# The first feature block's conditioning sums as matmuls with the conditioning column

## The chip, the cores and the metric

One NeuronCore of a Trainium2 chip runs the whole program in one launch. The metric is device time in microseconds of one execution; a number for a kernel is the median of several executions. The profile is one further execution, recorded with its own time.

## The reference

Two layers of an encoder trunk over a sequence of 1024 rows of 1024 features. What matters here is the start of the first layer: the input rows are normalized, scaled and shifted by vectors that depend on a conditioning vector `c`, and multiplied with `w_in`.

```python
def rmsnorm(x, g):
    xf = x.astype(jnp.float32)
    y = xf * lax.rsqrt(jnp.mean(xf * xf, axis=-1, keepdims=True) + NORM_EPS)
    return (y * g.astype(jnp.float32)).astype(x.dtype)

def modulate(h, shift, scale):
    return h * (1 + scale[:, None, :]) + shift[:, None, :]

c_act = jax.nn.silu(c)                         # 1024 numbers
...
    mod = c_act @ ada_w[l] + ada_b[l]          # 1024 x 6144
    sh_m, sc_m, g_m, sh_f, sc_f, g_f = jnp.split(mod, 6, axis=-1)
    h = modulate(rmsnorm(x, norm_g[l, 0]), sh_m, sc_m)
    if l < N_A:
        y = short_conv_mixer(h, conv_in_w[l], conv_w[l], conv_b[l], conv_out_w[l])
...
def short_conv_mixer(h, w_in, w_conv, b_conv, w_out):
    bcx = h @ w_in                             # 1024 x 1024 times 1024 x 3072
    b_gate, c_gate, xh = jnp.split(bcx, 3, axis=-1)
...
```

## The kernel before

Features are cut into eight blocks `k` of 128 (`KD = 8`), rows into eight tiles of 128, and the sequence into two halves of 512. `conv_phase` opens the program. Its first half loops over the eight feature blocks; for each block it needs three things on TensorE:

- The normalized rows of the block, turned to features by rows: `turn(k, half)` does four transposes of 128 x 128 into one PSUM tile `tp`. The rows come from `norm_x(0)`: for each of the four row tiles ACT squares and sums (`junk`, L364) and takes a root (L366), VectorE takes the reciprocal (L371) and scales the rows in place (`y`, L1175).
- The block's scale and shift, `sh[k]`, two columns of 128 numbers. They are sums over all 1024 conditioning numbers: `ada_cols` loads the block's columns of `ada_w` (tile `aw`, four DMAs of half the rows of either scale or shift), `ada_sum` multiplies and adds its eight row blocks with `csil`, the silu of `c`, in eight VectorE operations (L1083, then seven of L1085) into the tile `av`; `ada_end` sums `av` over its 128 partitions by a matmul with a column of `ones` (L1092, one for the scale and one for the shift), and two VectorE operations make `sh` of it (L1093, L1095). Blocks 0 and 1 have sums of their own, 256 wide; from block 2 on, two blocks share eight operations, 512 wide.
- The block's weights, `weights(k)`: 128 rows of `w_in` with 768 columns (tile `w`), split into a high and a low part by `split_w` (ACT L240, VectorE L241).

`scaled` then makes the block's operand: ACT writes it twice from `tp` (L1106), rounded into `slot` (hi) and in full into `q`; VectorE subtracts (L1107), which leaves the low part, lo. `products` multiplies weights and operand: three groups `g` for each of two output blocks `m`, each group three matmuls of 512 columns (low x high, high x low, high x high, through `mm`, L237). Between the two `m` of a block `k` stands `scales(k + 1)`, with its `ada_end` ahead of everything else in it.

The order on TensorE and on the SP queue is that of the code (`pinned`); on ACT it is that of the code in `norm_x(0)`. On VectorE the order is that of the code inside `beside`, and a scheduler's elsewhere. Each engine runs its instructions strictly in that order. SP issues the loads: `c`, four row tiles of `x`, then for blocks 0 and 1 `aw` and `w`, then two blocks at a time; `aw` has three buffers.

`c` is read as a column tile, element by element, into `craw` by the first DMA; ACT takes its exponential at once (L201) and VectorE makes `csil` of it. After Exp, ACT takes a first root (L228), so that its table for roots is there before `norm_x(0)`. Gains and biases come as rows (`vrows`, `brows`) and are turned by TensorE in `feature_rows` (L1059).

Of the kernel before, what the change touches and what calls it, by code (L numbers as in the profile page):

```python
# [8 lines left out]
F32 = mybir.dt.float32  # L9
# [3 lines left out]
ALU = mybir.AluOpType  # L13
# [4 lines left out]
P = 128  # L18
# [90 lines left out]
def trunk_kernel(ctx: ExitStack, tc: tile.TileContext, x, c, ada_w, ada_b, norm_g, conv_in_w, conv_w,  # L109
# [5 lines left out]
    def nm(s):  # L115
        uid[0] += 1
        return f"{s}_{uid[0]}"
# [73 lines left out]
    def ld(out_, in_):  # L191
        nc.sync.dma_start(out_, in_)
# [4 lines left out]

    csil = cp.tile([P, KD], F32, name="csil")
    craw = cp.tile([P, KD], F32, name="craw")
    ld(craw, c.rearrange("o (k p) -> p (o k)", p=P))  # L200
    nc.scalar.activation(csil, craw, AF.Exp, scale=-1.0)  # L201
    nc.scalar.dma_start(cs, consts[:, :C_T])

    rows_ = raw_tile()
    vrows, brows, mrows = (rows_[:, i * P:(i + 1) * P] for i in range(3))
    nc.scalar.dma_start(vrows[0:64, :], norm_g.rearrange("l v (k p) -> (l v k) p", p=P))
    nc.scalar.dma_start(brows[0:96, :], ada_b.rearrange("l (k p) -> (l k) p", p=P))

# [14 lines left out]
    nc.vector.memset(eps_d, D * EPS)  # L223
    eps_1 = cp.tile([P, 1], F32, name="eps_1")
    nc.vector.memset(eps_1, EPS)
    vecs = cp.tile([P, VEC_ROWS], F32, name="vecs")
    bias = cp.tile([P, BIAS_ROWS], F32, name="bias")
    nc.scalar.activation(bias[:, 0:1], csil[:, 0:1], AF.Sqrt)  # L228

    def gain(l, v):  # L230
        return vecs[:, (l * 4 + v) * 8:(l * 4 + v) * 8 + 8]

# [2 lines left out]
    def mm(out_, lhs, rhs, first, last, more=False):  # L235
        for i, (a, b) in enumerate(((1, 0), (0, 1), (0, 0))):
            nc.tensor.matmul(out_, lhs[a], rhs[b], start=first and i == 0, stop=last and i == 2, skip_group_check=more)  # L237
# [2 lines left out]
        nc.scalar.activation(hi, src, AF.Copy)  # L240
        nc.vector.tensor_tensor(lo, src, hi.bitcast(F32), op=ALU.subtract)  # L241


    nc.vector.tensor_scalar(csil, csil, 1.0, None, op0=ALU.add)
    nc.vector.reciprocal(csil, csil)
    nc.vector.tensor_tensor(csil, csil, craw, op=ALU.mult)

    def ada_room(accp):
        return accp.tile([P, D], F32, tag="acc", name=nm("acc"), bufs=1)
# [782 lines left out]
    def conv_phase():  # L1032
# [20 lines left out]
            for t in range(4 * half, 4 * half + 4):  # L1053
                ld(xt[t], x0[t * P:(t + 1) * P, :])

        def feature_rows(src, *dst):
            p_ = tp_ps()
            n = src.shape[0]
            nc.tensor.transpose(p_[:, :n], src, ident[:n, :n])  # L1059
            o = 0  # L1060
            for d in dst:
                nc.vector.tensor_copy(d, p_[:, o:o + d.shape[-1]])
                o += d.shape[-1]
# [5 lines left out]
        def ada_cols(ks):  # L1069

            n = len(ks)
            raw = [st.tile([P, KD * 2 * P], F32, tag="aw", name=nm("aw"), bufs=3).rearrange(
                "p (i j m) -> p i j m", i=KD // n, j=2) for _ in range(n)]
            q = KD // 2
            for i in (0, q):
                for j, col in enumerate((D, 0)):
                    ld(raw[i * (n - 1) // q][:, i % (KD // n):i % (KD // n) + q, j, :],
                       w0[i * P:(i + q) * P, col + ks[0] * P:col + (ks[-1] + 1) * P].rearrange("(k p) m -> p k m", p=P))
            return [raw[i * n // KD][:, i % (KD // n)] for i in range(KD)]

        def ada_sum(ks, raw):
            acc = st.tile([P, 4 * P], F32, tag="av", name=nm("av"), bufs=2)[:, :len(ks) * 2 * P].rearrange("p (j m) -> p j m", j=2)
            nc.vector.tensor_scalar(acc, raw[0], csil[:, 0:1], None, op0=ALU.mult)  # L1083
            for i in range(1, KD):
                nc.vector.scalar_tensor_tensor(acc, raw[i], csil[:, i:i + 1], acc, op0=ALU.mult, op1=ALU.add)  # L1085
            for n, k in enumerate(ks):
                sums_[k] = acc[:, :, n * P:(n + 1) * P]

        def ada_end(k):
            p_ = tp_ps()  # L1090
            for j in range(2):
                nc.tensor.matmul(p_[:, j:j + 1], sums_[k][:, j, :], ones[:, 0:1], start=True, stop=True)  # L1092
            nc.vector.scalar_tensor_tensor(sh[k][:, 0:1], p_[:, 0:1], g1[:, k:k + 1], b1[:, k:k + 1], op0=ALU.mult,  # L1093
                                           op1=ALU.add)
            nc.vector.tensor_tensor(sh[k][:, 1:2], p_[:, 1:2], bias[:, k:k + 1], op=ALU.add)  # L1095
# [25 lines left out]
        def weights_split(raw):  # L1121
            room = len(ws) in order[:FIRST_KEPT]
            w = [wr[room].tile([P, 6 * P], F32R, tag="w" + part_, name=nm("w"), bufs=FIRST_KEPT if room else KD - FIRST_KEPT)
                 for part_ in "hl"]
            split_w(w[0], w[1], raw)
            return w

        late = []

        def products(w, k, half, m, acc, first, last):  # L1130
            for g in (1, 0, 2):
                mm(acc[m, g], [q[:, (2 * g + m) * P:(2 * g + m + 1) * P] for q in w], ops[("1", "2")[k // 4] + ("1", "2")[half]][k % 4],
                   first, last)

        kept_rows = [None, None]

# [36 lines left out]
        def norm_x(half):  # L1173
            for t in range(4 * half, 4 * half + 4):
                nc.vector.tensor_scalar(xt[t], xt[t], rroot(squares(nx, xt[t])), None, op0=ALU.mult)  # L1175
# [6 lines left out]
        with pinned([mybir.EngineType.PE, mybir.EngineType.SP]):  # L1182
            load_x(0)
            wraws, sums_, ws, turned = [], {}, [], {}

            def fetch(*ks):
                raw = ada_cols(ks)
                wraws.extend(weights(k) for k in ks)
                return ks, raw

            aws = [fetch(0), fetch(1)]
            feature_rows(vrows[:64, :], vecs[:, :64])
            feature_rows(brows[:96, :], bias[:, :96])
            nc.vector.tensor_scalar(g1, gain(0, 0), RMS, None, op0=ALU.mult)
            nc.vector.scalar_tensor_tensor(b1, bias[:, 8:16], 1.0, g1, op0=ALU.add, op1=ALU.mult)
            with pinned([mybir.EngineType.Activation]):
                norm_x(0)

            def scales(k, beside=None):
                ada_end(k)  # L1200
                if beside:
                    with pinned([mybir.EngineType.DVE]):
                        beside()
                scaled(k, turned.pop(k), old(k), ("11", "21")[k // 4])
                ws.append(weights_split(wraws[k]))

            ada_sum(*aws[0])
            turned[0] = turn(0, 0)
            scales(0, lambda: ada_sum(*aws[1]))
            turned[1] = turn(1, 0)  # L1210
            acc = banks6()
            for k in range(KD):
                if k % 2 == 0 and k + 2 < KD:
                    ada_sum(*fetch(k + 2, k + 3))
                elif k + 2 == KD:
                    load_x(1)
                    later_rows()
                products(ws[k], k, 0, 0, acc, k == 0, k == KD - 1)
                if k + 1 < KD:
                    scales(k + 1)  # L1220
                else:
                    evict(0, 0, acc)
                    norm_x(1)
                products(ws[k], k, 0, 1, acc, k == 0, k == KD - 1)
                if k + 2 < KD:
                    turned[k + 2] = turn(k + 2, 0)
            evict(1, 0, acc)
            st.release()
            cB = pool("cB", "right")
            for n, t_ in zip(("t1", "t2"), slots_of(cB, 2)):  # L1230
                ops[n] = as_quarter(t_)
            ops["t3"], ops["t4"] = [], {}
            ready = []

            def next_half():
                k = order[len(ready)]
                second_half(k, turn(k, 1))
                ready.append(k)

            next_half()  # L1240
            next_half()
            acc = banks6()
            summed = 0
            for n, k in enumerate(order):
                products(ws[k], k, 1, 0, acc, n == 0, n == KD - 1)
                if len(ready) < KD:
                    next_half()
                elif n == KD - 2:
                    feature_rows(mrows[:VEC_ROWS - 64 + 16, :], vecs[:, 64:VEC_ROWS], bias[:, 96:BIAS_ROWS])
                products(ws[k], k, 1, 1, acc, n == 0, n == KD - 1)  # L1250
                if summed < 4 and summed in order[:n + 1] and summed + 4 in ready:
                    sums(summed)
                    summed += 1
                if n == FIRST_KEPT - 1:
                    wr.pop().release()
                    up = pool("up", "right")
                    begun = load_pair(conv_in_w[0], 4 + 1)
                    begun += (up_split(up, begun[0]),)
            for m in range(2):
                evict(m, 1, acc)  # L1260
# [746 lines left out]
```

## Time and profile before

| | us |
|---|---|
| median of 3 executions | 2083.88 (2081.64 to 2084.84) |
| the profiled execution | 2082.84 |
| its span in the trace | 2081.1 |
| first product (`one<-slot,w`, L237) starts | 20.61 |
| first half's last products of `mm<-slot,w` start | 65.71 |

The span is the time from the first to the last recorded instruction; 1.7 us of the execution lie around it. Granted clock over the span is 0.998. A row of the timeline has start, length, engine, line, operation, tiles (out<-in), shape and count, and in brackets how long the engine sat idle before it and what ended that. Rows that follow each other are merged, their length then reaching from the first one's start to the last one's end. One f32 matmul of 128 x 128 with one column leaves two records, so the two matmuls of an `ada_end` stand as `x4`. In rows of stages the numbers behind the length are busy time and count for each engine.

### The profile page before, as it was taken

To read this page: it belongs to the slowest core of one execution; us is meant where nothing else is said; L and a number is where in the kernel's file an instruction comes from. 1 tells how busy PE (TensorE), PEld (TensorE's weight loads), DVE (VectorE), ACT (ScalarE), POOL (GpSimd) and SP (SyncE) were. 2 spreads that over 40 slices of the span, in tenths; PEclk is the share of its full clock that TensorE was granted. 3 is DMA by queue.
4 is the path that set the end of the run, shared out by engine and by line. 5 is a ranking of instruction groups with operands and counts; after the bars stand their busy time and mean duration, and the time that the engine had idled before them with its cause. 6 is when DMAs were issued, how large, how long until landed. Compare 5 with 4: busy or idle time off the path is not lost.

```text
span 2081.1 us, 25026 instructions
## 1 busy us (share of the span) xinstructions
PE 2036.0 (98%) x9447; PEld 1683.6 (81%) x9447; DVE 1554.1 (75%) x2070; ACT 1083.9 (52%) x1547; POOL 5.3 (0%) x13
## 2 busy tenths in 40 slices
PE   6999999999999999999999999999999999999998
PEld 4788878878878788888878888888788888888886
DVE  7687877885776569978788978878976764567477
ACT  4642355754444434456775655657654454543443
POOL 0000000000000000000000000000000000000000
PEclk9999999999999999999999999999999999999999
DMA  9144465264664889756221212253354644774355
GB/s 306 31 152 140 151 217 169 93 198 161 213 196 167 279 271 325 232 181 221 74 76 59 69 55 89 82 168 141 117 193 165 204 157 171 241 256 146 109 171 175
DMA packets 241630, 344.46 MB, mean 166 GB/s; under 512 B 18949, under 2 KB 132962, under 8 KB 241510
## 3 DMA queue, kind: packets, MB, share of 16 engines
q1 hardware_dynamic: 199414, 253.84, 38.7%
q10 hardware_dynamic: 42096, 89.03, 11.6%
q8 instruction: 74, 1.21, 0.3%
q14 instruction: 46, 0.38, 0.1%
HBM read 258.94 MB, written 83.89 MB: 165 GB/s over the span
## 4 chain that ended last, share of the span: by engine, by line
PE 86%; DVE 7%; DMA 3%; ACT 3%; issue 1%; SPq 0%; ACTq 0%; DVEq 0%
PE one L237 41%; PE mm L237 22%; PE big L237 8%; PE tp L237 8%; PE big L1642 2%; DMA raw<-in_ada_w_dram 2%; PE tp L1679 1%; DVE small L1647 1%; PE tp L505 1%; DVE acc L273 1%; DMA raw<-ha 1%; DVE ring L241 1%; PE tp L566 0%; DVE p L1657 0%; DMA raw<-in_conv_out_w_dram 0%
## 5 line engine op out<-in xcount | busy, mean ns | idle before, releaser
L237 PE MATMUL one<-slot,uphi 128*128 128x512 f32 x1208 | 372.4, 390 | 0.0
L237 PE MATMUL one<-ring,ring 128*128 128x512 f32 x1152 | 262.9, 390 | 2.3 <-DVE ring L241 2.3
L237 PEld LDWEIGHTS one<-slot,uphi 128*128 128x128 f32 x1208 | 226.9, 188 | 46.9 <-issue 0.5
L237 PEld LDWEIGHTS one<-ring,ring 128*128 128x128 f32 x1152 | 216.0, 188 | 48.2 <-ACT ring L240 3.1
L237 PE MATMUL one<-slot,uplo 128*128 128x512 f32 x604 | 237.9, 394 | 7.3 <-ACT y L681 3.8
L241 DVE TENSOR_TENSOR ring<-raw,ring 128x1024 fp32r<-128x1024 f32 x144 | 174.4, 1220 | 55.9 <-ACT ring L240 55.6
L241 DVE TENSOR_TENSOR uplo<-raw,uphi 128x1024 fp32r<-128x1024 f32 x126 | 153.5, 1222 | 79.7 <-ACT uphi L240 79.7
L240 ACT ACTIVATE ring<-raw 128x1024 fp32r<-128x1024 f32 x144 | 149.4, 1051 | 105.8 <-DMA raw<-ha 64.8
L237 PE MATMUL mm<-ring,ring 128*128 128x512 f32 x768 | 185.0, 390 | 1.6 <-DVE ring L241 1.6
L240 ACT ACTIVATE uphi<-raw 128x1024 fp32r<-128x1024 f32 x126 | 132.2, 1056 | 102.0 <-PE one L237 25.7
L237 PE MATMUL tp<-ring,ring 128*128 128x512 f32 x768 | 184.0, 390 | 0.0
L240 ACT ACTIVATE ring<-w 128x1024 fp32r<-128x1024 f32 x80 | 84.7, 1059 | 168.8 <-PE tp L237 88.9
L237 PEld LDWEIGHTS mm<-ring,ring 128*128 128x128 f32 x768 | 143.8, 188 | 32.0 <-DVE ring L241 2.5
L237 PEld LDWEIGHTS tp<-ring,ring 128*128 128x128 f32 x768 | 144.2, 188 | 29.8
L241 DVE TENSOR_TENSOR ring<-w,ring 128x1024 fp32r<-128x1024 f32 x80 | 97.7, 1222 | 77.0 <-ACT ring L240 77.0
L273 DVE SCALAR_TENSOR_TENSOR acc<-raw,csil,acc 128x1024 f32<-128x1024 f32 x88 | 112.8, 1282 | 41.4 <-DMA raw<-in_ada_w_dram 37.0
L237 PEld LDWEIGHTS one<-slot,uplo 128*128 128x128 f32 x604 | 113.4, 188 | 35.1 <-ACT y L681 6.4
L237 PE MATMUL one<-slot,s 128*128 128x512 f32 x468 | 112.8, 390 | 0.2
L237 PE MATMUL mm<-slot,uphi 128*128 128x512 f32 x360 | 111.0, 390 | 0.0
L237 PEld LDWEIGHTS one<-slot,s 128*128 128x128 f32 x468 | 87.7, 188 | 19.2 <-DVE s L625 1.0
L237 PE MATMUL big<-slot,slot 128*128 128x512 f32 x384 | 96.1, 397 | 2.1 <-ACT y L1002 2.1
L237 PE MATMUL one<-q,uphi 128*128 128x512 f32 x312 | 96.2, 390 | 0.0
(353 smaller groups left out, 3546.0 us busy)
## 6 DMA issues: line engine op xcount, KB each, us to landing
ha<-y ACTq DMA_DIRECT2D x224, 256.0 KB, 2.4
raw<-ha SPq DMA_DIRECT2D x112, 512.0 KB, 4.1
raw<-in_ada_w_dram SPq DMA_DIRECT2D x80, 512.0 KB, 4.1
raw<-in_mlp_up_w_dram SPq DMA_DIRECT2D x72, 512.0 KB, 4.5
w<-in_mlp_down_w_dram SPq DMA_DIRECT2D x48, 512.0 KB, 6.5
raw<-in_mlp_down_w_dram SPq DMA_DIRECT2D x32, 512.0 KB, 4.3
xs<-raw ACTq DMA_DIRECT2D x19, 512.0 KB, 3.2
raw<-in_conv_in_w_dram SPq DMA_DIRECT2D x18, 512.0 KB, 4.9
```

The lines of the kernel that those rows point to most:

```text
L237: nc.tensor.matmul(out_, lhs[a], rhs[b], start=first and i == 0, stop=last and i == 2, skip_group_check=more)
L240: nc.scalar.activation(hi, src, AF.Copy)
L241: nc.vector.tensor_tensor(lo, src, hi.bitcast(F32), op=ALU.subtract)
L273: nc.vector.scalar_tensor_tensor(acc, raw, s, acc, op0=ALU.mult, op1=ALU.add)
L505: nc.tensor.transpose(p_[:, t * P:(t + 1) * P], ys[half * 4 + t][:, k * P:(k + 1) * P], ident)
L1642: nc.tensor.matmul(o_, a, m_, start=j == 0, stop=j == 4)
L1647: nc.vector.tensor_reduce(st["mx"], st["sp"][:, :n], AX.X, ALU.max, negate=True)
L1679: nc.tensor.transpose(p_[:, c:c + P], pts[h, 4 * hf + i][:, j * P:(j + 1) * P], ident)
```

## The change

Block 0 alone is handled in another way, and `c` is read in another form.

- `ada_sum` of block 0 goes. In `ada_end(0)` eight matmuls with the block's `aw` as weights and one column of `csil` as operand add up the scale in PSUM, and eight more the shift (16 matmuls for 2, and eight VectorE operations fewer).
- Block 0's weights `w` are loaded ahead of its `aw`, and its `aw` comes scale columns first, then shift columns. Block 0's `w` is split right behind `norm_x(0)`.
- `c` comes as eight rows of 128 beside the gains, and is turned with them by TensorE; silu reads the result from PSUM. A root of a constant (`eps_t`) stands behind Exp in the code.
- Block 0's products for the first half are in the order low x high for all three groups, then high x high, then high x low.

On VectorE, before, around the sums of blocks 0 to 2 (`av_225`, `av_244`, `av_281`; `sh_159` and `sh_160` are blocks 0 and 1):

```order
L1085 SCALAR_TENSOR_TENSOR av_225<-aw_171,csil,av_225 128x256 x3
L241 TENSOR_TENSOR w_257<-w_176,w_256 128x768
L1085 SCALAR_TENSOR_TENSOR av_225<-aw_171,csil,av_225 128x256 x2
L1093 SCALAR_TENSOR_TENSOR sh_159<-tp_239,g_157,b_158 128x1
L1095 TENSOR_TENSOR sh_159<-tp_239,bias 128x1
L1083 TENSOR_SCALAR av_244<-aw_178,csil 128x256
```

```order
L1083 TENSOR_SCALAR av_281<-aw_271,csil 128x512
L1085 SCALAR_TENSOR_TENSOR av_244<-aw_178,csil,av_244 128x256
L1085 SCALAR_TENSOR_TENSOR av_281<-aw_271,csil,av_281 128x512
L1093 SCALAR_TENSOR_TENSOR sh_160<-tp_299,g_157,b_158 128x1
L1085 SCALAR_TENSOR_TENSOR av_281<-aw_271,csil,av_281 128x512
L1095 TENSOR_TENSOR sh_160<-tp_299,bias 128x1
```

And now (`sh_155`, `sh_156` are blocks 0 and 1, `av_255` and `av_288` the sums of block 1 and of blocks 2 and 3):

```order
L1195 TENSOR_SCALAR y_148<-y_148,small_224 128x1024
L239 TENSOR_TENSOR w_228<-w_167,w_227 128x768
L1107 SCALAR_TENSOR_TENSOR sh_155<-tp_236,g_153,b_154 128x1
L1109 TENSOR_TENSOR sh_155<-tp_236,bias 128x1
L1093 TENSOR_SCALAR av_255<-aw_174,csil 128x256
L1095 SCALAR_TENSOR_TENSOR av_255<-aw_174,csil,av_255 128x256
L1121 TENSOR_TENSOR slot_131<-q_138,slot_131 128x512
L1095 SCALAR_TENSOR_TENSOR av_255<-aw_174,csil,av_255 128x256 x5
L239 TENSOR_TENSOR w_315<-w_179,w_314 128x768
```

```order
L1107 SCALAR_TENSOR_TENSOR sh_156<-tp_306,g_153,b_154 128x1
L1109 TENSOR_TENSOR sh_156<-tp_306,bias 128x1
L1093 TENSOR_SCALAR av_288<-aw_278,csil 128x512
L1095 SCALAR_TENSOR_TENSOR av_288<-aw_278,csil,av_288 128x512
```

Block 0's sums are gone from VectorE, and the sums of blocks 2 and 3, three of which stood ahead of block 1's finished `sh`, now all stand behind it. From `sh` of block 2 on, the five queues hold the same rows in the same order as before.

On TensorE, before, from the last of block 0's transposes to its first products:

```order
L1100 MATMUL tp_234<-cs,y_152 128x128
L1092 MATMUL tp_239<-ones,av_225 128x1 x2
L1100 MATMUL tp_260<-cs,y_149 128x128
```

And now:

```order
L1114 MATMUL tp_231<-cs,y_148 128x128
L1104 MATMUL tp_236<-csil,aw_169 128x1 x16
L1114 MATMUL tp_267<-cs,y_145 128x128
```

The 16 matmuls stand where the two stood, behind the four transposes, of which the last needs the fourth row tile scaled.

On ACT, before, from the first table load to the first root of `norm_x(0)`:

```order
L201 ACT_TABLE_LOAD
L201 ACTIVATE csil<-craw 128x8
L228 ACT_TABLE_LOAD
L228 ACTIVATE bias<-csil 128x1
L364 ACTIVATE junk_193,small_194<-y_149 128x1024
L366 ACTIVATE small_196<-small_194,eps_d 128x1
```

And now:

```order
L244 ACT_TABLE_LOAD
L244 ACTIVATE eps_t<-eps_d 128x1
L242 ACT_TABLE_LOAD
L242 ACTIVATE csil<-tp_181 128x8
L365 ACTIVATE junk_195,small_196<-y_145 128x1024
L367 ACT_TABLE_LOAD
L367 ACTIVATE small_198<-small_196,eps_d 128x1
```

The scheduler put the root of the constant ahead of Exp, which waits for TensorE; a third table load stands ahead of the first root.

The diff:

```diff
-    ld(craw, c.rearrange("o (k p) -> p (o k)", p=P))
-    nc.scalar.activation(csil, craw, AF.Exp, scale=-1.0)
...
+    ld(vrows[64:64 + KD, :], c.rearrange("o (k p) -> (o k) p", p=P))
...
-    nc.scalar.activation(bias[:, 0:1], csil[:, 0:1], AF.Sqrt)
...
-    nc.vector.tensor_scalar(csil, csil, 1.0, None, op0=ALU.add)
-    nc.vector.reciprocal(csil, csil)
-    nc.vector.tensor_tensor(csil, csil, craw, op=ALU.mult)
+    def silu(p_):
+        nc.scalar.activation(csil, p_, AF.Exp, scale=-1.0)
+        nc.vector.tensor_copy(craw, p_)
+        nc.scalar.activation(eps_t, eps_d, AF.Sqrt)
+        nc.vector.tensor_scalar(csil, csil, 1.0, None, op0=ALU.add)
+        nc.vector.reciprocal(csil, csil)
+        nc.vector.tensor_tensor(csil, csil, craw, op=ALU.mult)
...
+            if ks == (0,):
+                raw = st.tile([P, KD * 2 * P], F32, tag="aw", name=nm("aw"), bufs=3).rearrange("p (j i m) -> p i j m", i=KD, j=2)
+                for j, col in enumerate((D, 0)):
+                    for i in (0, KD // 2):
+                        ld(raw[:, i:i + KD // 2, j, :],
+                           w0[i * P:(i + KD // 2) * P, col:col + P].rearrange("(k p) m -> p k m", p=P))
+                return [raw[:, i] for i in range(KD)]
...
             for j in range(2):
-                nc.tensor.matmul(p_[:, j:j + 1], sums_[k][:, j, :], ones[:, 0:1], start=True, stop=True)
+                if k == 0:
+                    for i, raw in enumerate(aws[0][1]):
+                        nc.tensor.matmul(p_[:, j:j + 1], raw[:, j, :], csil[:, i:i + 1], start=i == 0, stop=i == KD - 1)
+                else:
+                    nc.tensor.matmul(p_[:, j:j + 1], sums_[k][:, j, :], ones[:, 0:1], start=True, stop=True)
...
+            if half == 0 and first:
+                for i, (a, b) in enumerate(((1, 0), (0, 0), (0, 1))):
+                    for g in (1, 0, 2):
+                        nc.tensor.matmul(acc[m, g], lhs[g][a], rhs[b], start=i == 0, stop=False)
+                return
...
-            aws = [fetch(0), fetch(1)]
-            feature_rows(vrows[:64, :], vecs[:, :64])
+            wraws.append(weights(0))
+            aws = [((0,), ada_cols((0,))), fetch(1)]
+            feature_rows(vrows[:64 + KD, :], vecs[:, :64], more=silu)
...
             with pinned([mybir.EngineType.Activation]):
                 norm_x(0)
+                ws.append(weights_split(wraws[0]))
...
-                ws.append(weights_split(wraws[k]))
+                if k:
+                    ws.append(weights_split(wraws[k]))
...
-            ada_sum(*aws[0])
             turned[0] = turn(0, 0)
             scales(0, lambda: ada_sum(*aws[1]))
```

More of the change, by code (lines that the diff above doesn't have):

```diff
@@ L225, in trunk_kernel @@
     nc.vector.memset(eps_1, EPS)
+    eps_t = cp.tile([P, 1], F32, name="eps_t")
     vecs = cp.tile([P, VEC_ROWS], F32, name="vecs")
     bias = cp.tile([P, BIAS_ROWS], F32, name="bias")
-    nc.scalar.activation(bias[:, 0:1], csil[:, 0:1], AF.Sqrt)
     def gain(l, v):
@@ L1054, in load_x, with feature_rows @@
                 ld(xt[t], x0[t * P:(t + 1) * P, :])
-        def feature_rows(src, *dst):
+        def feature_rows(src, *dst, more=None):
             p_ = tp_ps()
@@ L1059, in feature_rows @@
             nc.tensor.transpose(p_[:, :n], src, ident[:n, :n])
+            if more:
+                more(p_[:, n - KD:n])
             o = 0
@@ L1130, in products @@
         def products(w, k, half, m, acc, first, last):
+            rhs = ops[("1", "2")[k // 4] + ("1", "2")[half]][k % 4]
+            lhs = {g: [q[:, (2 * g + m) * P:(2 * g + m + 1) * P] for q in w] for g in range(3)}
+            if half == 0 and first:
[3 more added lines that the diff above has]
+                return
             for g in (1, 0, 2):
-                mm(acc[m, g], [q[:, (2 * g + m) * P:(2 * g + m + 1) * P] for q in w], ops[("1", "2")[k // 4] + ("1", "2")[half]][k % 4],
-                   first, last)
+                mm(acc[m, g], lhs[g], rhs, first, last)
         kept_rows = [None, None]
```

## The prediction, on record before the changed kernel ran

> **What bounds the kernel now.** I read the page's shares first, then busy time by stage, the chain of waits up to 45 us and the timeline from 2 to 34 us; after 68 us the change moves nothing.
>
> ```profile
> PE 2036.0 (98%) x9447; PEld 1683.6 (81%) x9447; DVE 1554.1 (75%) x2070; ACT 1083.9 (52%) x1547; POOL 5.3 (0%) x13
> ...
> PE 86%; DVE 7%; DMA 3%; ACT 3%; issue 1%; SPq 0%; ACTq 0%; DVEq 0%
> ```
>
> Over the whole span TensorE sets the time, so a delay of its start is paid once, at the end. The first 34 us are another matter. Busy time by stage (length, then PE, PEld, DVE, ACT, POOL busy with counts, granted clock, DMA share, GB/s):
>
> ```profile
> 19.60:33.30 13.70, 11.39 (x45) 8.64 (x46) 13.12 (x28) 5.09 (x7) 0.00 (x0) 1.00 1.05 335
> 33.30:67.30 34.00, 32.28 (x159) 25.92 (x159) 23.79 (x45) 19.29 (x32) 0.00 (x0) 1.00 0.51 171
> ```
>
> From 19.6 to 33.3 us VectorE is busy 13.12 of 13.70 us and is the bound; from 33.3 on TensorE is (32.28 of 34.00). The chain (start, length, what) goes from VectorE's sums to the small matmul and on to `sh`:
>
> ```profile
> 18.34 1.03 PE tp L1092 x4
> ...
> 19.53 0.15 DVE sh L1095
> ...
> 31.49 0.75 DVE av L1085
> ...
> 32.38 0.58 PE tp L1092 x4
> ```
>
> So I follow one quantity: when `sh` of blocks 0, 1 and 2 is ready. Before, that is at 19.68, 26.98 and 33.30 us (19.53 + 0.15, 26.83 + 0.15 and 0.28 after 33.02, below).
>
> **Term 1, ACT's tables.** In the built order the sqrt warm-up stands first, then Exp, so the first root of norm_x needs a third table load, behind the first square.
>
> ```profile
> 3.92 1.28 ACT L228 ACT_TABLE_LOAD   x1
> ...
> 5.21 0.20 ACT L228 ACTIVATE bias<-csil 128x1 f32<-128x1 f32 x1
> ...
> 6.71 1.06 ACT L364 ACTIVATE junk<-y 128x1024 bf16<-128x1024 f32 x1 [1.29 <-DMA y<-in_x_dram]
> ...
> 7.89 0.29 ACT L366 ACTIVATE small<-small,eps_d 128x1 f32<-128x1 f32 x1
> ...
> 8.22 0.16 DVE L371 RECIPROCAL small<-small 128x1 f32<-128x1 f32 x1 [0.16 <-ACT small L366]
> 8.42 0.75 DVE L1175 TENSOR_SCALAR y<-y,small 128x1024 f32<-128x1024 f32 x1
> ...
> 12.09 0.29 ACT L366 ACTIVATE small<-small,eps_d 128x1 f32<-128x1 f32 x1
> ...
> 14.10 0.75 DVE L1175 TENSOR_SCALAR y<-y,small 128x1024 f32<-128x1024 f32 x1
> ...
> 14.90 0.48 PE L1100 MATMUL tp<-cs,y 128*128 128x128 f32 x1 [2.42 <-DVE y L1175]
> ```
>
> A load takes 1.28 us and the next ACTIVATE starts 0.01 behind it (3.92 to 5.21). The four roots run from 7.89 to 12.09, 1.40 apart. After: first root 7.89 + 1.29 = 9.18, fourth 13.38; the last row scale 0.33 + 0.20 later (as 8.42 behind 7.89), 13.91 to 14.66; last transpose 14.71. Before it stood at 14.90, since that scale, free from about 12.6, was queued behind sums until 14.10. So the load costs nothing: the removed sums were the delay that covers it. Without that cover it would be 1.29. The Trainium skill (ScalarE: Activation LUTs, What ACT_TABLE_LOAD costs) adds a drain of 1.38 us to each load; no drain shows beside the loads of this trace, and by the page the sum would be about 1.4 higher.
>
> **Term 2, block 0's sums on TensorE.** VectorE loses eight operations, the last of which ended at 18.3. TensorE gains 16 matmuls of one column, in program order behind the four transposes.
>
> ```profile
> 12.79 0.35 DVE L1083 TENSOR_SCALAR av<-aw,csil 128x256 f32<-128x256 f32 x1 [0.83 <-DMA aw<-in_ada_w_dram]
> ...
> 15.54 0.84 ACT L240 ACTIVATE w<-w 128x768 fp32r<-128x768 f32 x1 [3.15 <-DMA w<-in_conv_in_w_dram]
> ...
> 18.34 0.37 PE L1092 MATMUL tp<-ones,av 128*128 128x1 f32 x1 [2.96 <-DVE av L1085]
> ...
> 18.34 1.02 PE L1092 MATMUL tp<-ones,av 128*128 128x1 f32 x4 [2.96 <-DVE av L1085]
> ...
> 22.16 3.50 PE L237 MATMUL one<-slot,w 128*128 128x512 f32 x8 [0.76 <-DVE slot L1107]
> ...
> 26.64 1.55 PE L237 MATMUL mm<-slot,w 128*128 128x512 f32 x6
> ...
> 32.38 0.58 PE L1092 MATMUL tp<-ones,av 128*128 128x1 f32 x4 [0.96 <-DVE av L1085]
> ```
>
> ```profile
> L1092 PE MATMUL tp<-ones,av 128*128 128x1 f32 x32 | 4.6, 248 | 3.9 <-DVE av L1085 3.9
> ```
>
> The same form (128x128 f32 weights, one column) is there at two speeds. Two instructions make four records: at 18.34 they start (1.02 - 0.37) / 3 = 0.217 us apart, at 32.38, with the mean of one at 248 ns, (0.58 - 0.25) / 3 = 0.11. The products tell why: eight take 3.50 us at 22.16 (0.44 each), six 1.55 at 26.64 (0.26). The array runs at half speed until about 25 us. Bounds for 32 records: 31 x 0.11 + 0.25 = 3.7 us and 31 x 0.217 + 0.37 = 7.1. Up to 14.9 TensorE does little but transposes, as it did up to 18.34, so I take 7.1. They start at 14.71 + 0.23 (a transpose's share) = 14.94 and end at 22.04. Data don't bind: w and block 0's four pieces of `aw` carry the same bytes in the other order and are all there by about 15.5, as w was; the last piece is wanted near 20.
>
> ```profile
> 19.53 0.15 DVE L1095 TENSOR_TENSOR sh<-tp,bias 128x1 f32<-128x1 f32 x1
> 19.60 0.34 DVE L1083 TENSOR_SCALAR av<-aw,csil 128x256 f32<-128x256 f32 x1
> ...
> 19.78 0.78 ACT L1106 ACTIVATE slot<-tp,sh 128x512 fp32r<-128x512 f32 x1 [3.40 <-DVE sh L1095]
> ...
> 20.45 0.77 ACT L1106 ACTIVATE q<-tp,sh 128x512 f32<-128x512 f32 x1
> ...
> 21.42 0.69 DVE L1107 TENSOR_TENSOR slot<-q,slot 128x512 fp32r<-128x512 f32 x1
> ...
> 22.02 0.48 DVE L1085 SCALAR_TENSOR_TENSOR av<-aw,csil,av 128x256 f32<-128x256 f32 x1
> ...
> 23.28 1.00 DVE L1085 SCALAR_TENSOR_TENSOR av<-aw,csil,av 128x256 f32<-128x256 f32 x2
> 24.20 0.48 DVE L1083 TENSOR_SCALAR av<-aw,csil 128x512 f32<-128x512 f32 x1
> ...
> 26.17 0.75 DVE L1085 SCALAR_TENSOR_TENSOR av<-aw,csil,av 128x512 f32<-128x512 f32 x1
> ...
> 26.83 0.15 DVE L1095 TENSOR_TENSOR sh<-tp,bias 128x1 f32<-128x1 f32 x1
> ...
> 29.17 1.53 DVE L1085 SCALAR_TENSOR_TENSOR av<-aw,csil,av 128x512 f32<-128x512 f32 x2
> ...
> 32.15 0.95 DVE L241 TENSOR_TENSOR w<-w,w 128x768 fp32r<-128x768 f32 x1
> ...
> 33.02 0.21 DVE L1093 SCALAR_TENSOR_TENSOR sh<-tp,g,b 128x1 f32<-128x1 f32 x1
> ```
>
> From the small matmuls' end (18.34 + 1.02) to `sh` ready are 0.32 us, so block 0 has it at 22.36 against 19.68: **+2.7**. Meanwhile VectorE, done with the split of w0 near 15.6, waits: block 1's sums are queued in it behind `sh`, though their data are in.
>
> **Term 3, what fills VectorE's waits.** Before, three of block 2's eight sums (24.20, one near 25.2, 26.17) ran ahead of block 1's `sh`; now all eight stand behind it. Counted from 22.36: block 1's two first sums, then lo waits for q (0.10 + 0.67 + 0.77 us behind `sh`, and 0.03), so it starts at 23.93; 0.60 to the next (21.42 to 22.02), five sums at 0.50 (two in 1.00 at 23.28) 27.0, split 0.87 (32.15 to 33.02), last sum 0.50, small matmuls 0.58 and 0.04, `sh` 0.34: 29.3, before 26.98 (+2.3). Block 2: lo at 29.3 + 1.57 = 30.9, 0.60, five sums at 0.76 (two in 1.53) 35.3, split 0.87, the last sum 0.66 (26.17 to 26.83), second split 0.87, `sh` 0.28: 37.9, before 33.30, **+4.6** in all. Term 3 alone is +2.0 of it.
>
> **Term 4, block 0's products.** Six of nine now need `hi` alone, so TensorE's 0.76 us ahead of the products at 22.16 goes. It is worth nothing: TensorE next waits for block 1's sums until 28.4, and nine products at 0.44 are done by 27.3.
>
> **Term 5, conditioning as rows.** One DMA of 8 rows takes the place of one of 1024 elements. At best x lands sooner: ACT waited 1.29 for it at 6.71. Bounds 0 and -1.2; x's own 512 KB pieces still have to come, so I take -0.2, near the first.
>
> From block 2's `sh` on every queue holds the same order as before and both engines meet there with the same backlog, so the offset stays. Sum: 4.6 - 0.2 = **+4.4 us**. The profiled execution took 2082.84, 1.04 below the median of 2083.88; on the mean of the four executions shown, 2083.3, the forecast is 2087.7.
>
> **Rivals.** (B) The array comes to full speed in the midst of the 16 matmuls. Later in this trace it fell to half and rose again:
>
> ```profile
> 284.60:288.00 3.40, 1.34 (x6) 0.80 (x6) 3.40 (x4) 2.25 (x3) 0.00 (x0) 1.00 0.85 288
> 288.00:291.40 3.40, 3.40 (x9) 2.62 (x9) 1.50 (x2) 2.42 (x3) 0.00 (x0) 0.50 0.99 370
> ```
>
> A stretch of 3.4 us with 1.34 busy was followed by one at clock 0.50, and that, fully busy, by full clock. If 3.4 us of one-column matmuls count as busy, 16 records go at 0.217 and 16 at 0.11: 1.7 us less, +2.7, 2086.0. Against it: the mixture of such matmuls and transposes from 18.34 on left the array at half speed at 22.16. The rule that some 3.4 us of sustained work brings the full clock is also in the Trainium skill (TensorE: Matmul & The Clock Gate, Part 1); the rows above agree with it, but no run here shows what a one-column matmul counts for.
>
> (C) The loss is given back between 33 and 67 us: TensorE is idle there 1.7 us, and if it never had to wait, the end would be +2.7, or +1.0 along with B. Against it: the same orders, so the same waits.
>
> (D) Not slower: the 16 matmuls run at 0.11 from the first and x lands 1.2 us sooner, so they end at 14.94 - 1.2 + 3.7 = 17.4 and `sh` at 17.8: -1.9 + 2.0 of term 3, 2083.3. It becomes faster than before once block 0's `sh` is ready before 17.7. Against it: 0.217 at 18.34.
>
> (E) Worse: the array is still slow at block 1's sums (0.4) or the load carries over a microsecond more: to 2089.3.
>
> **How the numbers follow.** Chances: forecast 0.46, B 0.24, C 0.10, D 0.11, E 0.09. The range of 2083.6 to 2089.4 leaves out half of D and half of E. About 0.2% (4.2 us) is what a measurement can tell from no change, and the forecast's +4.4 lies just past it: slower is some 0.27 of the forecast's 0.46, E and a little of B, 0.40; faster is half of D and a little unknown, 0.07; the rest, 0.53, is within.
>
> **What would show it.** In the changed trace: a table load between the first square and root near 7.9; 32 records about 0.22 apart from 14.9 to 22.0 (B: they come closer half way); VectorE idle from 15.6 until `sh` near 22; block 1's `sh` at 29.3 and block 2's at 37.9; from there on everything as before, 4 to 5 us later. I am wrong if TensorE is fast by then, or if the offset at 38 us is not the offset at the end.

## The result, and the profile after

| | before | after |
|---|---|---|
| median, us | 2083.39 (2081.64 to 2084.84, 4 executions) | 2102.77 (2101.41 to 2105.86, 4 executions) |
| ratio to before, 95% interval | | 1.0096 (1.0085 to 1.0108) |
| the profiled execution, us | 2082.84 | 2101.41 |
| its span, us | 2081.1 | 2099.5 |

The changed kernel is 19.4 us slower; the forecast was 4.4 us slower, and the range ended at 2089.4. The shares of the page, then busy time by stage (the first row's stage runs from the first products to block 2's `sh`):

```profile
PE 2059.1 (98%) x9475; PEld 1688.8 (80%) x9475; DVE 1552.3 (74%) x2063; ACT 1085.5 (52%) x1548; POOL 5.3 (0%) x13
...
PE 83%; DVE 7%; DMA 5%; ACT 3%; issue 1%; ACTq 0%; DVEq 0%; SPq 0%
```

```profile
20.60:36.71 16.11, 12.41 (x46) 9.53 (x46) 13.71 (x28) 5.10 (x7) 0.00 (x0) 0.89 0.77 251
36.71:68.00 31.29, 29.53 (x146) 23.67 (x145) 23.09 (x45) 17.53 (x30) 0.00 (x0) 1.00 0.55 185
```

TensorE is busy 23.1 us longer than before (2059.1 against 2036.0) with 28 records more. The 16 new matmuls, 6.8 us for the 1.0 of the two that they replace, explain 5.8 us of that. The rest is what the forecast did not have.

The start came out nearly as forecast. The timeline of the changed kernel:

```profile
5.67 1.05 ACT L365 ACTIVATE junk<-y 128x1024 bf16<-128x1024 f32 x1
...
6.83 1.28 ACT L367 ACT_TABLE_LOAD   x1
8.12 0.29 ACT L367 ACTIVATE small<-small,eps_d 128x1 f32<-128x1 f32 x1
...
13.56 0.48 PE L1114 MATMUL tp<-cs,y 128*128 128x128 f32 x1 [0.89 <-DVE y L1195]
13.83 6.83 PE L1104 MATMUL tp<-csil,aw 128*128 128x1 f32 x32
...
20.69 0.22 DVE L1107 SCALAR_TENSOR_TENSOR sh<-tp,g,b 128x1 f32<-128x1 f32 x1 [6.32 <-PE tp L1104]
20.82 0.15 DVE L1109 TENSOR_TENSOR sh<-tp,bias 128x1 f32<-128x1 f32 x1
...
27.89 0.15 DVE L1109 TENSOR_TENSOR sh<-tp,bias 128x1 f32<-128x1 f32 x1
...
36.56 0.15 DVE L1109 TENSOR_TENSOR sh<-tp,bias 128x1 f32<-128x1 f32 x1
```

The third table load stands behind the first square, the 32 records take 6.83 us, VectorE is idle for 6.32 us until they end, and `sh` of blocks 0, 1 and 2 is ready at 20.97, 28.04 and 36.71 us (before: 19.68, 26.98, 33.30). At block 2 the two traces are 3.4 us apart, and so they are still at 54 and at 70 us. Then the distance grows, although every queue holds the same rows: 3.9 us at 100 us of the trace of before, 4.8 at 150, 6.2 at 240, 9.6 at 500, 12.5 at 850, 18.6 at 1750, 18.9 from 1780 to 2040 and 18.5 at the last product. No wait on TensorE was added: it is idle for 40.4 us of the span (2099.5 - 2059.1), where it was for 45.1 before (2081.1 - 2036.0). The products themselves stand further apart. Four rows of the same place in both traces, before and then after (start, length of the merged records):

```profile
479.81 0.39 PE L237 MATMUL one<-q,uplo 128*128 128x512 f32 x1
480.03 0.62 PE L237 MATMUL one<-q,uphi 128*128 128x512 f32 x2
480.49 0.39 PE L237 MATMUL one<-q,uplo 128*128 128x512 f32 x1
480.71 0.62 PE L237 MATMUL one<-q,uphi 128*128 128x512 f32 x2
```

```profile
489.04 0.40 PE L235 MATMUL one<-q,uplo 128*128 128x512 f32 x1
489.27 0.63 PE L235 MATMUL one<-q,uphi 128*128 128x512 f32 x2
489.74 0.40 PE L235 MATMUL one<-q,uplo 128*128 128x512 f32 x1
489.97 0.63 PE L235 MATMUL one<-q,uphi 128*128 128x512 f32 x2
```

Three products take 0.68 us before (479.81 to 480.49) and 0.70 after (489.04 to 489.74): 227 ns each against 233. Not all products are slower. Groups of the page's kind (busy us, mean ns of one), before and then after:

```profile
L237 PE MATMUL one<-slot,uphi 128*128 128x512 f32 x1208 | 372.4, 390 | 0.0
L237 PE MATMUL one<-ring,ring 128*128 128x512 f32 x1152 | 262.9, 390 | 2.3 <-DVE ring L241 2.3
...
L237 PE MATMUL one<-q,uphi 128*128 128x512 f32 x312 | 96.2, 390 | 0.0
```

```profile
L235 PE MATMUL one<-slot,uphi 128*128 128x512 f32 x1208 | 376.1, 392 | 0.0
L235 PE MATMUL one<-ring,ring 128*128 128x512 f32 x1152 | 263.0, 390 | 2.2 <-DVE ring L239 2.2
...
L235 PE MATMUL one<-q,uphi 128*128 128x512 f32 x312 | 97.9, 395 | 0.0
```

`ring` times `ring` is as before; `slot` or `q` times `uphi` is slower. What separates them is where the tiles lie. The program places tiles in a partition from two ends: `slot`, `q` and the vectors of the start from the left, `ring`, `uphi` and `uplo` from the right (and some of the `slot` tiles). The change's new one-column tile `eps_t` takes 32 bytes in the left side's first pool, so all left tiles behind it move by 32 bytes and the right ones do not. The tiles' addresses in the built programs show it. Before, both operands of nearly every 512-column product have the same remainder modulo 256 bytes, 224. After, a left operand has remainder 0 and a right one still 224; `one<-q,uphi` pairs the two in all its 312 products, `one<-ring,ring` never.

### The profile page after: what moved, and what is told of

Same layout as the page of the kernel before. It is cut to its first block, busy times and chain, and to the rows that moved or that the text cites. A ratio compares the mean times of both kernels' runs of the same rounds, so it can differ in the third digit from the quotient of the medians.

```text
span 2099.5 us, 25072 instructions
## 1 busy us (share of the span) xinstructions
PE 2059.1 (98%) x9475; PEld 1688.8 (80%) x9475; DVE 1552.3 (74%) x2063; ACT 1085.5 (52%) x1548; POOL 5.3 (0%) x13
## 4 chain that ended last, share of the span: by engine, by line
PE 83%; DVE 7%; DMA 5%; ACT 3%; issue 1%; ACTq 0%; DVEq 0%; SPq 0%
PE one L235 40%; PE mm L235 22%; PE big L235 8%; PE tp L235 7%; PE big L1664 3%; DMA raw<-ha 2%; DMA raw<-in_ada_w_dram 1%; PE tp L1701 1%; DVE ring L239 1%; DVE small L1669 1%; DVE acc L274 1%; PE tp L506 1%; DMA raw<-in_kv_ada_w_dram 1%; ACT ring L238 0%; DMA raw<-in_conv_out_w_dram 0%
## 5 line engine op out<-in xcount | busy, mean ns | idle before, releaser
L239 DVE TENSOR_TENSOR ring<-raw,ring 128x1024 fp32r<-128x1024 f32 x144 | 174.4, 1220 | 57.0 <-ACT ring L238 56.8
```

## The experiments

Theory A: the addresses make the products slower, and the change's own work costs only the start. Rival B: the instructions do (the new order, or something that they leave behind). Each ratio is to the kernel before, run in the same series: its median was 2083.13 us for e1 to e4, 2081.87 for e5 to e8 and 2082.16 for e9 to e12.

**The old addresses, and the shift alone.** Two kernels swap the suspected cause between before and after. e1 is the changed kernel without an unused 32-byte tile that stands ahead of `eps_t`, so the tiles behind `eps_t` are back where they were:

```diff
-    cp.tile([P, 8], F32, name="even")
```

> The changed kernel without the unused 32-byte tile `even`: every tile from `vecs` on lies where it lay before the change; the instructions are the changed kernel's. Theory A (the 32 bytes that `eps_t` pushes everything else up by cost some 16 us, and the start of the kernel 3.4 us, which is the offset of block 2's `sh`): 2083.4 + 3.4 = 2086.8, between 2085.5 and 2088.5; products of the MLP 227 ns apart again. Rival B (what slows the products is in the changed instructions, say 28 more TensorE instructions and the order they are fetched in): stays at 2102 to 2104.

e2 is the kernel before with an unused tile in the place of `eps_t`:

```diff
+    cp.tile([P, 1], F32, name="eps_t")
     vecs = cp.tile([P, VEC_ROWS]...
```

> The kernel before with one unused column tile where the change has `eps_t`; no instruction differs. Theory A: 2083.4 + 16 = 2099, between 2096 and 2102, slower by 0.6 to 0.9%. Rival B: 2083.4, no change.

Measured: e1 2088.08 us, ratio 1.0029 (1.0019 to 1.0038); e2 2097.04, ratio 1.0071 (1.0054 to 1.0088), where no instruction of the change is in it. In e1's trace the slower groups have their old busy times back:

```profile
L234 PE MATMUL one<-slot,uphi 128*128 128x512 f32 x1208 | 372.1, 389 | 0.0
...
L234 PE MATMUL one<-q,uphi 128*128 128x512 f32 x312 | 96.1, 389 | 0.0
```

In e2's trace TensorE is busy 17.1 us longer than before (2053.1 against 2036.0), and the groups that grew are those of the changed kernel:

```profile
L238 PE MATMUL one<-slot,uphi 128*128 128x512 f32 x1208 | 376.1, 392 | 0.0
L238 PE MATMUL one<-ring,ring 128*128 128x512 f32 x1152 | 263.0, 390 | 2.2 <-DVE ring L242 2.2
...
L238 PE MATMUL one<-q,uphi 128*128 128x512 f32 x312 | 97.9, 395 | 0.0
```

These three are the changed kernel's busy times to the tenth. B falls, A stands.

**Which property of the address.** Either the two sides must match (A1), or one remainder is good in itself and another is bad (A2). e3 is the changed kernel with an unused 32-byte tile at the start of the right side too; e4 is the kernel before with that tile alone. Its edit:

```diff
+    padr = pool("padr", "right")
+    padr.tile([P, 8], F32, name="padr")
     nx = pool("nx", "right")
```

> The changed kernel with a further 32 bytes set aside at the other end of the memory, so that tiles of both sides lie at multiples of 64 bytes. Theory A1 (a product is slow where the operand that streams and the weights that load lie at different remainders of 64 bytes, 0 and 32): both sides agree again, 2086 to 2089. Rival A2 (a remainder of 0 is slow in itself, for whichever tile): as slow as the changed kernel or slower, 2102 to 2110, since the tiles of the down projections now lie there too.

> The kernel before with the 32 bytes at the other end alone; no instruction differs. Left tiles stay at remainder 32, right tiles go to 0. A1: products with one operand of each side slow down, as in the changed kernel, 2096 to 2102. A2: products with any right tile slow down, the down projections' too, whose operands are both on the right: more than A1, 2100 to 2115. Rival B: 2083.4.

Measured: e3 2099.23, ratio 1.0080 (1.0065 to 1.0095), in neither forecast; e4 2097.98, ratio 1.0070 (1.0055 to 1.0085). e4 shows that moving the right side costs what moving the left one does. A1 with a period of 64 bytes fell with e3, where both sides have remainder 0 modulo 64. So did A2, which had the products of `ring` with `ring` slow there; they take what they took before:

```profile
L235 PE MATMUL one<-ring,ring 128*128 128x512 f32 x1152 | 263.0, 390 | 2.3 <-DVE ring L239 2.3
```

The right side had moved down where the left had moved up, so in e3 the two are 64 bytes apart. That left a match with a longer period.

**The period.** e5 and e9 are the kernel before with an unused tile of 128 and of 256 bytes in `eps_t`'s place (`cp.tile([P, 32], ...)`, `cp.tile([P, 64], ...)`).

> The kernel before, with an unused tile of 128 bytes per partition in the place of eps_t: every left-side tile moves by 128 bytes instead of 32, and nothing else changes. A1 refined (a product is slow where the address of its moving operand and that of the weights loaded beside it differ modulo 128 bytes): the two sides agree modulo 128 as before, so spacing stays at 227 ns and the time at 2083 (within 2 us of before). A3 (any shift of the left side against the right breaks something that was tuned, such as a larger period or a collision at one place): some 227 to 233 ns in the up-projections as in the changed kernel, +14 us, 2097.

> The kernel before with an unused tile of 256 bytes per partition in the place of eps_t. The two sides then differ by 256 bytes modulo 512. If the period of the match is 256 bytes: 227 ns and 2082 to 2084. If it is 512 or more, a part of the loss stays, less than the +9.6 us that 128 bytes cost (products across the two sides near 229 to 231 ns): 2085 to 2090. If any shift counts in full: 2097.

Measured: e5 2091.49, ratio 1.0045 (1.0029 to 1.0060), between the two forecasts; e9 2082.05, ratio 0.9998 (0.9989 to 1.0007).

**Both sides moved together.** e10 is the kernel before without the unused tile on the left (left side 32 bytes down) and with `padr` (right side 32 bytes down): every address behind them differs from before, no difference between the sides does.

> The kernel before without its unused tile 'even' (the left side moves down by 32 bytes) and with an unused tile of 32 bytes at the start of the right side (which moves it down by 32 bytes too): all addresses change, the difference between the sides doesn't. If only the match of a product's two operands counts: 227 ns everywhere, 2082 to 2084. If the remainder itself counts (480 of 512 before, now 448): the same-side products slow down too, 2097 or more.

Measured: 2082.47, ratio 1.0004 (0.9995 to 1.0013). So it is the difference that counts, and 256 bytes are as good as none. The groups of e9, then of e10:

```profile
L238 PE MATMUL one<-slot,uphi 128*128 128x512 f32 x1208 | 373.3, 390 | 0.0
```

```profile
L236 PE MATMUL one<-slot,uphi 128*128 128x512 f32 x1208 | 372.1, 389 | 0.0
```

Taken together, from the start times of all 512-column products that follow each other from 70 us on, with spacings of 200 to 260 ns, parted by how far the address of a product's moving operand and that of the next product's weights (whose load runs beside it) lie apart modulo 256 bytes:

| kernel | match: mean spacing, products | no match: bytes apart, mean spacing, products | PE busy, us |
|---|---|---|---|
| before | 227.12 ns, 7676 | | 2036.0 |
| e9, left 256 bytes | 227.11 ns, 7669 | | 2037.3 |
| e10, both sides 32 bytes | 227.15 ns, 7680 | | 2037.0 |
| e2, left 32 bytes | 227.96 ns, 5587 | 32, 233.31 ns, 2086 | 2053.1 |
| e4, right 32 bytes | 227.94 ns, 5589 | 32, 233.30 ns, 2093 | 2052.4 |
| e5, left 128 bytes | 227.44 ns, 5596 | 128, 232.52 ns, 2093 | 2047.3 |
| after | 227.96 ns, 5590 | 32, 233.32 ns, 2092 | 2059.1 |
| e3, after, both sides | 228.16 ns, 5596 | 64, 230.88 ns, 2093 | 2055.5 |
| e11, after, addresses of before | 227.14 ns, 7685 | | 2042.4 |

The loss of the changed kernel follows from its row: 2092 x (233.32 - 227.12) = 13.0 us and 5590 x (227.96 - 227.12) = 4.7 us, 17.7 in all, where the busy time says 16.7 (2059.1 - 2042.4). The spans of the two traces differ by less, 12.7 us (2099.5 - 2086.8), since TensorE is also idle for 4.0 us less (40.4 against 44.4). Nearly all products here match both their own weights and the next ones, or neither. An exception are 58 products of the groups `big<-slot` and `big<-slot,slot`, which match their own and, once one side has moved, not the next ones. Their mean spacing is 227.0 ns before, 232.7 in e2, 232.6 in e4, 232.9 after and 232.3 in e5, so at 32 and at 128 bytes the next product's weights are what must match. In e3, 64 bytes apart, the same 58 are at 228.4, no slower than the others of their groups (228.9), and there it stays open. It was not tried why matching products are 0.8 ns slower beside others that do not match.

**The change without the shift.** e11 has every instruction of the change and every address of before: the root of the constant goes to a column of the unused tile.

```diff
-    cp.tile([P, 8], F32, name="even")
+    even = cp.tile([P, 8], F32, name="even")
...
-    eps_t = cp.tile([P, 1], F32, name="eps_t")
+    eps_t = even[:, 0:1]
```

> The changed kernel, whose only edit is that the root of the constant goes to a column of the unused tile 'even' instead of a tile of its own: every instruction of the change, every address of before. Only the start then costs: +3.4 to 3.6 us of block 2's shift to the end, 2085 to 2088. If the address was not the cause of the rest: 2097 to 2103.

Measured: 2086.88 us (2084.74 to 2090.59), ratio 1.0023 (1.0014 to 1.0032), which is 4.8 us over before with an interval of 2.9 to 6.7. Its trace is 3.7 us behind that of before at block 2's `sh` (36.87 + 0.15 = 37.02 against 33.30) and still 3.7 at 240 us:

```profile
14.14 6.83 PE L1104 MATMUL tp<-csil,aw 128*128 128x1 f32 x32
```

```profile
36.87 0.15 DVE L1109 TENSOR_TENSOR sh<-tp,bias 128x1 f32<-128x1 f32 x1
```

**What of the start costs it.** Three kernels on the base of e1, each with one part changed. e6 puts block 0's sums back on VectorE (`ada_sum(*aws[0])` and two matmuls with `ones`); weights first, rows of `c` and the order of the products stay.

> The changed kernel on the old addresses (without the unused tile 'even'), with block 0's sums back on VectorE (16 one-column matmuls become 2, eight VectorE operations come back); weights first, scale columns first, conditioning as rows and the product order stay. If the 16 matmuls and what they leave on VectorE (terms 2 and 3) are what the start still costs: block 2's finished shift about 33.3 less 1.0 (x lands sooner) plus 0 to 1.3 (table load without its cover), so 32.3 to 33.6 instead of 36.7, and 2082 to 2084, no slower than before. Rival (the order of loads or the rows cost it): it stays at 36 to 37 us, and 2087 to 2088.

Measured: 2083.51, ratio 1.0009 (1.0001 to 1.0018). Block 2's `sh` is ready at 34.35 us (34.20 + 0.15), a little later than expected but 2.5 us sooner than in e1 (36.66 + 0.15), and the time 4.2 us lower (0.20% of 2083): the matmuls, with what they leave undone on VectorE, are most of the cost of the start.

e7 reads `c` as a column again, with Exp and the first root as before.

> The changed kernel on the old addresses, with the conditioning read element by element as a column again, Exp and the first root as before; the 16 matmuls stay. By the traces the rows let x land 1.04 us sooner and cost a third table load of 1.28 us behind the first square. If the load is on the path of the 16 matmuls (nothing queued ahead of the last row scale any more), the column loses 1.04 and gains 1.28: block 2's shift at 36.5 to 37, 2087 to 2089, no change to e1's 2088. If the load is covered, as term 1 had it: 37.7, and 2089 to 2090.

Measured: 2088.14, ratio 1.0026 (1.0013 to 1.0039), no change that can be measured against e1's 1.0029. Its trace answers two questions:

```profile
5.79 1.06 ACT L363 ACTIVATE junk<-y 128x1024 bf16<-128x1024 f32 x1 [0.37 <-DMA y<-in_x_dram]
...
12.73 6.83 PE L1102 MATMUL tp<-csil,aw 128*128 128x1 f32 x32
...
35.98 0.14 DVE L1107 TENSOR_TENSOR sh<-tp,bias 128x1 f32<-128x1 f32 x1
```

x landed early here too, so the rows are not what brought it. And without the third table load the 16 matmuls start 1.19 us sooner than in e1 (12.73 against 13.92), and block 2's `sh` is ready 0.69 sooner (36.12 against 36.81). The load lies on the path. Neither expectation had both, an early x with the column and a load that costs.

e8 lets block 1's eight sums run on VectorE ahead of block 0's `sh`, where it was idle for 6.32 us.

```diff
-            scales(0, lambda: ada_sum(*aws[1]))
+            with pinned([mybir.EngineType.DVE]):
+                ada_sum(*aws[1])
+            with behind(last_dve()):
+                scales(0)
```

> The changed kernel on the old addresses, with block 1's eight sums put ahead of block 0's two operations for its shift on VectorE, where VectorE is idle for 6.3 us. If term 3 (the wait that nothing fills) is the cost: the sums run from about 14 to 20 us, within the idle time; block 0's shift is as in the changed kernel, near 21.0, block 1's some 4 us sooner (about 24), block 2's at 32 to 33.5, and the time 2082 to 2084, no slower than before. Rival (the late small matmuls of block 0 alone bind, since TensorE is then behind): block 2's shift near 36, and 2086 to 2088.

```profile
16.37 0.35 DVE L1092 TENSOR_SCALAR av<-aw,csil 128x256 f32<-128x256 f32 x1 [1.80 <-DMA aw<-in_ada_w_dram]
16.76 3.61 DVE L1094 SCALAR_TENSOR_TENSOR av<-aw,csil,av 128x256 f32<-128x256 f32 x7
20.89 0.22 DVE L1106 SCALAR_TENSOR_TENSOR sh<-tp,g,b 128x1 f32<-128x1 f32 x1 [0.53 <-PE tp L1103]
...
26.29 0.15 DVE L1108 TENSOR_TENSOR sh<-tp,bias 128x1 f32<-128x1 f32 x1
...
31.82 0.15 DVE L1108 TENSOR_TENSOR sh<-tp,bias 128x1 f32<-128x1 f32 x1
```

Block 2's `sh` is ready at 31.97 us, 4.8 sooner than in e1 and 1.3 sooner than before. Block 1's is ready at 26.44, not near 24. Its `aw` landed at 16.37 only, but its sums are done by 20.4, ahead of block 0's `sh`. What it waits for is TensorE, whose order puts block 1's small matmuls behind nine products of block 0, the first of them still at half speed:

```profile
22.11 3.67 PE L1149 MATMUL one<-slot,w 128*128 128x512 f32 x9
25.62 0.50 PE L1105 MATMUL tp<-ones,av 128*128 128x1 f32 x4
```

The time is 2083.99, ratio 1.0010 (1.0001 to 1.0019): 4.0 us below e1's ratio, so term 3 was a real cost that a filled wait gives back. It does not beat before.

e12 has both e8's and e7's edits on the addresses of before.

> The changed kernel on the addresses of before, with block 1's eight sums ahead of block 0's finished shift on VectorE (the start 4.2 us sooner at 240 us than with the sums behind it, in the traces so far) and the conditioning read as a column (0.7 us sooner). If both add: block 2's shift at 31 to 32 us against 33.3, the offset at 240 us -1 to -2, and 2080 to 2082, 1 to 2 us faster than before, about what a measurement can tell. Rival: what is gained at the start is lost to stretches of half clock later, or is hidden: within 1 us of before, or up to 2 us slower, as the fill alone was.

Measured: 2081.94, ratio 0.9999 (0.9991 to 1.0008). The time lies in both forecasts; that it is no faster than before is the rival's. Block 2's `sh` is at 32.70 us (32.55 + 0.15) and the trace 0.6 us ahead of before at 240 us, less than the first forecast had: block 1's `aw` landed at 16.92, so its sums, though queued first, began only then, and block 0's `sh` behind them came at 21.11, although the 16 matmuls had ended at 19.62. No version here beats the kernel before by more than its measurement can tell.

## Why the prediction was wrong

**The step that failed** is the last of its sum: "From block 2's `sh` on every queue holds the same order as before and both engines meet there with the same backlog, so the offset stays". The order was the same and the offset did not stay. Of the 19.4 us, some 15 (the ratios of the changed kernel and of e11, 1.0096 and 1.0023, are 0.73% apart, and e2, the shift alone, costs 0.71%) are slower products, 6 ns each where the operands no longer match, because a tile of 32 bytes moved one operand against the other. No rival had it; all five cases priced instructions and waits alone. The prediction named the right sign, "if the offset at 38 us is not the offset at the end", without a mechanism behind it. The chance of 0.53 for no measurable change went with it.

**The start was right in its sum, by e11**: +4.8 us (2.9 to 6.7) measured, +4.4 forecast. Over the traces whose start has the same instructions, block 2's `sh` is ready at 32.09 to 33.35 us with those of before (six, mean 32.95) and at 36.71 to 37.10 with those of after (four, mean 36.91), 4.0 us apart. Its terms:

- Term 1, the table load, said to cost nothing. A load without a drain beside it was seen (6.83 to 8.12, then the root at 8.12). Against before it is covered, as reckoned, but in the changed kernel the cover is gone: e7, without it, starts the 16 matmuls 1.19 us sooner and reaches block 2's `sh` 0.69 us sooner.
- Term 2, the 16 matmuls: 7.1 us taken for 32 records, 6.83 measured; they begin right behind the last transpose, as told. From the first square to `sh` of block 0 are 15.30 us (5.67 to 20.97), where the working had 15.65 (6.71 to 22.36).
- Term 3, VectorE's empty wait: from block 0's `sh` to block 2's the working had 15.5 us (22.36 to 37.9), the trace has 15.74 (20.97 to 36.71). e8 confirms the cause.
- Term 4 worth nothing: nine products end at 25.60 (21.91 + 3.69) and TensorE then waits 1.54 us for block 1's sums, at the small matmuls of 27.14.
- Term 5, the rows, taken as -0.2 of a possible -1.2. In the one changed profile x seemed to land 1.04 us sooner (first square at 5.67 against 6.71). Over the traces of all kernels here the first square starts at 5.45 to 6.71 us with the column (eight, mean 5.93) and at 5.61 to 5.99 with the rows (six, mean 5.76): the profile of before that the forecast stood on had the latest of all. The -0.2 agrees with the means, and one trace's DMA landing was no ground for either number.

**Rival B**, full speed half way through the matmuls, did not come: the merged row of 32 records has the length of 31 x 0.21 + 0.35, and the nine products behind it still take 3.69 us (0.41 each, where products stand 0.23 apart later). The rule of the Trainium skill (TensorE: Matmul & The Clock Gate, Part 1), that sustained work of about 4 us brings the full clock, did not hold for one-column matmuls here: 6.83 us of them did not. **Rival C**, the loss given back, did not come either, as e11 ends 4.8 us late. **Rival D** (x 1.2 us sooner, the matmuls at 0.11) had x nearly right, by chance, and the matmuls wrong. **E** is the end that would have been nearest, at 2089.3, for another reason.

## What to carry to other kernels

A new tile is part of a change even when nothing reads it in a hot loop: it moves all that is placed behind it. Before forecasting "the rest stays as it was", compare addresses as well as orders; where two operands come from pools at opposite ends, keep their difference a multiple of 256 bytes here, or let the new value live in a spare column. When a loss grows evenly along the trace with no new wait, look at the spacing of equal instructions, not at the dependencies.

## What the hardware showed that was not expected

- A product of 512 columns (nearly all of them fp32r in the program, f32 in the profile) was 227.1 ns from the next when the moving operand's address and that of the weights loaded beside it agreed modulo 256 bytes, 233.3 ns when they were 32 bytes apart, 230.9 at 64 and 232.5 at 128. Other distances and other types were not tried.
- A stretch with little work on TensorE was followed by half the clock, here as at 284.6 us before. In the changed kernel (length, busy PE, PEld, DVE, ACT, POOL, granted clock, DMA share, GB/s):

```profile
24.80:28.20 3.40, 1.86 (x11) 1.32 (x10) 2.60 (x7) 0.07 (x1) 0.00 (x0) 1.00 0.46 146
28.30:31.70 3.40, 3.40 (x12) 2.60 (x11) 2.93 (x5) 2.75 (x4) 0.00 (x0) 0.50 0.95 317
```

A stretch of 3.4 us in which TensorE is busy for 1.86, waiting for block 1's sums, is followed by 3.4 us at half clock for block 1's products. It cost nothing that the trace shows, since TensorE waits for the next sums anyway (1.78 us, until 35.80). It is why the clock column of the stage 20.60 to 36.71 reads 0.89.
- Executions of one kernel spread by 7 us here (before: 2078.73 to 2086.13 in 33). In the traces, stretches of 3.4 us at half clock fall at 288, 625 or 1220 us in some and not in others, each worth about 1.7 us by estimate (half of 3.4); e8's trace has two of them, where that of before has one, and is behind at its end although it was 0.7 us ahead at 240 us. That they make up the whole spread was not tested.
